# Sixteen weight units split ahead in mixer blocks one and two of a hybrid decoder layer

## The chip, the cores and the metric

The kernel runs on one core of one Trainium2 chip. The metric is the device time of one execution in microseconds (us). Five engines matter: TensorE (PE, with its weight loads as PEld), VectorE (DVE), ScalarE (ACT), GpSimd (POOL) and SyncE (SP), whose queue issues nearly all DMAs. Each engine and each queue takes its instructions in the order in which the program lists them.

## The reference

One layer of a hybrid decoder on a prompt of 2048 tokens and a sample of 8 x 4 tokens, with 1024 features:

```python
xr, gate, q, k, v = jnp.split(rmsnorm(x, g_mix) @ w_in, SPLITS, axis=-1)
y_lru = rg_lru(causal_dwconv(xr, ...), ...) * gelu(gate)       # 512 wide
y_att = sliding-window attention with sinks over q, k, v       # 512 wide
x = x + concat([y_lru, y_att]) @ w_out                         # 1024 x 1024
qc = rmsnorm(x, g_cross) @ w_mem_q                             # 1024 x 512
x = x + softmax(qc mem_k^T / sqrt(128)) mem_v @ w_mem_o        # 512 x 1024
x = x + ConvFFN(rmsnorm(x, g_ffn)); y = rmsnorm(x, ...)
```

`w_in` gives 1792 columns; the memory attention has 4 heads over 256 memory tokens. Outputs are the two y, new caches and states.

## The kernel before, in words

**Arithmetic.** Every product is made of three matmuls in fp32r: high by high, low by high, high by low (`mm3`, L137). So each operand is split: the high part is a rounding copy (ScalarE, L79), the low part the difference (L83, on GpSimd for weights, on VectorE for most activations).

**Stages.** The tokens go in four blocks of 512 (the last one is 544 with the sample). Phase 0 makes the memory keys and values (to 47 us in the profiled execution). Phase 1, the mixer, runs blocks 0 to 3 one after the other (block 1 from about 186 to 300 us, block 2 from 305 to 420, block 3 to 573); each has 14 units `unit(0)` to `unit(13)` of the input projection `w_in` (k, v, four of q, then xr and gate by turns; PSUM tile `pin`), with the window attention (`sc` scores, `tp` transposes, `po`) and the RG-LRU in between. The RG-LRU of one block is finished during the next: ScalarE makes exponentials and roots, GpSimd the products `lu` (L970), VectorE the scan (L989), GpSimd `hlast` and `gate` (L990, L991), and the result goes by DMA to `ymix` in DRAM (L996). Phase 2 (573 to about 1077 us) takes a block's `ymix` back, does the output projection (eight units of `w_out`, `out(0)` to `out(7)`, PSUM tile `po2`), the norm (`x`, `xgh`, `xgl`), the memory queries (four units of `w_mem_q`, tile `pq`), the attention and four units of `w_mem_o`, each block overlapped with the next one's output projection. Phase 3 is the ConvFFN (to the end at 2744 us).

**Weights.** A unit is 128 x 1024. `weight_order` (L85) lists all uses of phases 0 to 2 in order, and `weights` (L106) keeps two units ahead. The first time a unit is used it is loaded raw (`wr`, a pool of four buffers), split into `wh` (ScalarE) and `wl` (GpSimd), and, if it is used again, both parts are stored in DRAM (`keeph`, `keepl`, L127). At later uses the two parts are loaded (L119). The split parts lie in a pool `wspl` of three buffers for each of `wh` and `wl`, used in turn: a new tile goes into a buffer when its last reader is done. All of `w_in` is made in block 0 and reloaded in blocks 1 to 3; `w_out`, `w_mem_q` and `w_mem_o` are made when phase 2's first block reaches them, and reloaded for its other three blocks.

**Order.** A scheduler with a cost model sets the order on each engine before the run, from the order of the code and priorities; it also picks which buffer of a pool a tile takes.

Of the kernel before, what the change touches and what calls it, by code (L numbers as in the profile page):

```python
# [10 lines left out]
F = mybir.dt.float32  # L11
R = mybir.dt.float32r
# [33 lines left out]
class _Kernel:  # L46
# [38 lines left out]
    def weight_order(self):  # L85
        I = self.I
        o = [I["w_mem_k"][h] for h in range(4)] + [I["w_mem_v"][u] for u in range(4)]
        for s in range(4):
            o += [I["w_in"][u] for u in range(14)]
        o += [I["w_out"][m] for m in range(8)]  # L90
        for s in range(4):
            o += [I["w_mem_q"][h] for h in range(4)]
            if s < 3:
                o += [I["w_out"][m] for m in range(4)]
            o += [I["w_mem_o"][u] for u in range(4)]
            if s < 3:
                o += [I["w_out"][m] for m in range(4, 8)]
        self.worder, self.wq = o, []
        self.wsplit = 0
        self.wkey = lambda a: (a.tensor.name, a.offset)  # L100
        self.wkept = {}
        self.wuses = {}
        for a in o:
            self.wuses[self.wkey(a)] = self.wuses.get(self.wkey(a), 0) + 1

    def weights(self, src, ahead=2):  # L106


        nc = self.nc
        i = self.wsplit - len(self.wq)  # L110
        assert self.wkey(self.worder[i]) == self.wkey(src)
        while self.wsplit <= min(i + ahead, len(self.worder) - 1):
            unit = self.worder[self.wsplit]
            key = self.wkey(unit)
            hi = self.wspl.tile([128, 1024], R, name="wh", tag="wh")
            lo = self.wspl.tile([128, 1024], R, name="wl", tag="wl")
            if key in self.wkept:
                for t, d in zip((hi, lo), self.wkept[key]):
                    nc.sync.dma_start(t.bitcast(F), d)  # L119
            else:  # L120
                raw = self.wraw.tile([128, 1024], F, name="wr", tag="wr")
                nc.sync.dma_start(raw, unit)
                self.split(raw, hi, lo, "act", "pool" if self.wsplit > 2 else "dve")
                if self.wuses[key] > 1:
                    self.wkept[key] = [self.dram.tile([128, 1024], F, name=f"keep{e}{self.wsplit}") for e in "hl"]
                    for t, d in zip((hi, lo), self.wkept[key]):
                        nc.sync.dma_start(d, t.bitcast(F))  # L127
            self.wq.append((hi, lo))
            self.wsplit += 1
        return self.wq.pop(0)  # L130

    def mm3(self, outs, w, x, first, last, more=False):
        nc = self.nc
        combos = ((0, 0), (0, 1), (1, 0))
        for n, (a, b) in enumerate(combos):
            for o, xs in zip(outs, x[b]):
                nc.tensor.matmul(o, w[a], xs, start=first and n == 0, stop=last and n == 2, skip_group_check=more)  # L137
# [244 lines left out]
    def p1_block(self, s):  # L382
        nc, tc, I, O = self.nc, self.tc, self.I, self.O
# [10 lines left out]
        def unit(u):  # L394
            wt = self.weights(I["w_in"][u])
            ps = [self.psum([128, n], "mm", "pin") for _, n in subs]
            self.proj(wt, nh, nl, ps, subs, KT)
            return ps

        if s:  # L400
            nc.vector.tensor_copy(kh[:, 0:128], kh[:, 512:640].bitcast(F))
            nc.vector.tensor_copy(kl[:, 0:128], kl[:, 512:640].bitcast(F))
        ps = unit(0)
        if 0 < s < 3:
            self.p1_sums(s + 1)
# [4 lines left out]
        if smp:  # L410
            kf = q1.tile([128, 160], F, name="kf")
            nc.vector.tensor_copy(kf, ps[1][:, 384 - subs[1][0]:W - subs[1][0]])
            nc.sync.dma_start(O["swa_k"], kf[:, 0:128])
            nc.sync.dma_start(O["s_k_new"], kf[:, 128:160])
        ps = unit(1)
        next(fin, None)
        vt = q1.tile([128, W], F, name="vt")
# [6 lines left out]
        for j in range(4):  # L424
            ps = unit(2 + j)
            if j == 3 and s == 0:
                self.p1_sums(1)
                self.rts[1] = self.p1_rstd(1)
            h = q1.tile([128, W], R, name=f"qh{j}")
            l = q1.tile([128, W], R, name=f"ql{j}")  # L430
            for (o, n), p in zip(subs, ps):
                self.last_lo = self.split(p, h[:, o:o + n], l[:, o:o + n])
            if smp:
                f = q1.tile([128, NS], F, name=f"qf{j}")
                nc.vector.tensor_copy(f, ps[1][:, subs[1][1] - NS:subs[1][1]])
                qs.append(f)
            qh.append(h)
            ql.append(l)
            next(fin, None)
# [1167 lines left out]
```

## Time and profile before

| | |
|---|---|
| Time, median of 3 runs (lowest, highest) | 2738.78 us (2737.75, 2747.58) |
| Profiled execution: time | 2745.93 us |
| Profiled execution: span | 2744.2 us (1.7 us lie beside it) |
| TensorE busy, of the span | 2611.7 us, 95% |
| VectorE, ScalarE, GpSimd busy | 55%, 40%, 35% |
| TensorE's mean granted clock | 0.977 of full |

The profiled execution is 7.15 us longer than the median and 1.65 us shorter than the longest of the three. Times in the rows below are us from the span's start. A granted clock of 1.00 is the upper of TensorE's two levels (2.4 GHz), 0.50 the lower (1.2 GHz); a figure between them is a mean over a stretch.

### The profile page before, as it was taken

The numbers are of one execution on the slowest core, as the hardware profiler recorded it, in microseconds if no ns is written. First come the engines' busy times: TensorE is split into PE (matmuls) and PEld (weight loads), VectorE is DVE, ScalarE is ACT, GpSimd is POOL, SyncE is SP. The second block draws the span as 40 slices with busy tenths as digits, with TensorE's granted clock in tenths as the row PEclk, the third lists the DMA queues.
The fourth block names the chain that finished last, engine by engine and source line by source line (L and its number), as shares of the span: only waits on it lengthen the run. The fifth ranks groups of instructions, "written<-read, shape, count | busy, mean of one in ns | idle before, by whom it ended". The sixth has DMA issues, their size and how long they took to land.

```text
span 2744.2 us, 40972 instructions
## 1 busy us (share of the span) xinstructions
PE 2611.7 (95%) x15221; PEld 2407.4 (88%) x15221; DVE 1518.5 (55%) x2633; ACT 1085.6 (40%) x2071; POOL 954.5 (35%) x928
## 2 busy tenths in 40 slices
PE   7999999998999998888999999999999989999997
PEld 5778888977998887888999998899999989999997
DVE  6476766585442525767676755454444444444445
ACT  5454745474332434443334343333232323232233
POOL 2422211031402344466333344553232424333333
PEclk8899999998999999999999999999999999999998
DMA  6674545366747788766444487764444765444442
GB/s 234 241 230 168 183 158 173 109 243 245 258 165 245 255 268 306 272 242 209 183 161 177 146 314 252 254 216 162 150 160 158 289 214 164 159 158 167 149 154 83
DMA packets 195671, 553.72 MB, mean 202 GB/s; under 512 B 28628, under 2 KB 49364, under 8 KB 192784
## 3 DMA queue, kind: packets, MB, share of 16 engines
q1 hardware_dynamic: 195472, 551.10, 57.9%
q8 instruction: 120, 1.97, 0.3%
q14 instruction: 79, 0.65, 0.1%
HBM read 409.22 MB, written 141.80 MB: 201 GB/s over the span
## 4 chain that ended last, share of the span: by engine, by line
PE 69%; DVE 11%; DMA 6%; issue 4%; ACT 4%; POOL 4%; SPq 1%; POOLq 0%; DVEq 0%; ACTq 0%
PE pg L137 23%; PE pd L137 17%; PE pin L137 10%; PE po L137 5%; PE pmo L137 3%; PE pq L137 3%; DVE gc L1398 3%; POOL pc L83 2%; PE sc L137 1%; DMA x<-x2d 1%; ACT gc L1396 1%; DMA opd<-n3s 1%; POOL x L756 1%; POOL n3s L83 1%; PE tp L853 1%
## 5 line engine op out<-in xcount | busy, mean ns | idle before, releaser
L137 PE MATMUL pg<-n,pc 128*128 128x346 f32 (+1 forms) x6048 | 1022.0, 327 | 48.2 <-DVE up L1353 16.1
L137 PEld LDWEIGHTS pg<-n,pc 128*128 128x128 f32 x6048 | 965.6, 189 | 92.6 <-DVE up L1353 28.2
L83 POOL TENSOR_TENSOR pc<-wr,pc 128x512 fp32r<-128x512 f32 x312 | 411.0, 1322 | 451.4 <-ACT pc L79 446.2
L137 PE MATMUL pd<-ah,pc 128*128 128x346 f32 (+1 forms) x2240 | 467.7, 325 | 18.7 <-DVE acc L1422 12.9
L137 PEld LDWEIGHTS pd<-ah,pc 128*128 128x128 f32 x2240 | 379.4, 191 | 24.7 <-DVE acc L1422 17.6
L79 ACT ACTIVATE pc<-wr 128x512 fp32r<-128x512 f32 x312 | 195.3, 629 | 503.3 <-PE pd L137 236.7
L1422 DVE TENSOR_TENSOR acc<-pd,acc 128x692 f32<-128x692 f32 (+1 forms) x280 | 245.0, 878 | 175.6 <-PE pd L137 172.7
L137 PE MATMUL pd<-al,pc 128*128 128x346 f32 (+1 forms) x1120 | 271.6, 324 | 0.0
L137 PEld LDWEIGHTS pd<-al,pc 128*128 128x128 f32 x1120 | 196.6, 191 | 0.0
L1398 DVE SCALAR_TENSOR_TENSOR gc<-gb,pp,gc 128x696 f32<-128x696 f32 (+2 forms) x144 | 150.1, 1043 | 82.8 <-ACT gc L1396 79.0
L137 PE MATMUL pin<-n1h,wh 128*128 128x512 f32 (+1 forms) x560 | 188.9, 363 | 5.6 <-DVE ql L83 1.8
L137 PE MATMUL pin<-n1h,wl 128*128 128x512 f32 (+1 forms) x560 | 185.8, 358 | 2.8 <-POOL wl L83 2.8
L137 PE MATMUL pin<-n1l,wh 128*128 128x512 f32 (+1 forms) x560 | 186.6, 359 | 1.5 <-DVE n1l L83 1.5
L83 POOL TENSOR_TENSOR wl<-wr,wh 128x1024 fp32r<-128x1024 f32 x35 | 84.7, 2426 | 218.7 <-ACT wh L79 190.8
L1353 DVE TENSOR_TENSOR u<-pg,u 128x346 f32<-128x346 f32 (+1 forms) x144 | 74.3, 516 | 141.0 <-PE pg L137 140.5
L83 POOL TENSOR_TENSOR pc<-ws,pc 128x512 fp32r<-128x512 f32 x72 | 94.5, 1312 | 158.7 <-ACT pc L79 140.6
L1353 DVE TENSOR_TENSOR up<-pg,u 128x346 f32<-128x346 f32 (+1 forms) x144 | 74.1, 515 | 123.5 <-PE pg L137 123.5
L79 ACT ACTIVATE pc<-ws 128x512 fp32r<-128x512 f32 x144 | 90.0, 627 | 113.1 <-PE pg L137 70.0
L137 PEld LDWEIGHTS pin<-n1h,wh 128*128 128x128 f32 x560 | 103.1, 193 | 23.5 <-DVE ql L83 2.4
L1353 DVE TENSOR_TENSOR gb<-pg,u 128x314 f32<-128x314 f32 (+2 forms) x96 | 38.9, 426 | 145.5 <-PE pg L137 145.5
L137 PEld LDWEIGHTS pin<-n1h,wl 128*128 128x128 f32 x560 | 102.6, 193 | 18.8 <-POOL wl L83 3.8
L137 PEld LDWEIGHTS pin<-n1l,wh 128*128 128x128 f32 x560 | 102.7, 194 | 17.1 <-DVE n1l L83 2.6
(317 smaller groups left out, 4196.0 us busy)
## 6 DMA issues: line engine op xcount, KB each, us to landing
pc<-kept_s SPq DMA_DIRECT2D x192, 512.0 KB, 4.3
kept_s<-pc SPq DMA_DIRECT2D x96, 512.0 KB, 3.0
wh<-keeph SPq DMA_DIRECT2D x90, 512.0 KB, 4.0
wl<-keepl SPq DMA_DIRECT2D x90, 512.0 KB, 5.0
wr<-in_w_gate_dram SPq DMA_DIRECT2D x72, 512.0 KB, 3.8
wr<-in_w_down_dram SPq DMA_DIRECT2D x72, 512.0 KB, 4.0
opd<-n3s SPq DMA_DIRECT2D x56, 346.0 KB, 3.6
n<-opd SPq DMA_DIRECT2D x14, 1384.0 KB, 11.2
```

The lines of the kernel that those rows point to most:

```text
L79: nc.scalar.activation(hi, src, AF.Copy)
L83: return e.tensor_tensor(out=lo, in0=src, in1=hi.bitcast(F), op=OP.subtract).ins
L137: nc.tensor.matmul(o, w[a], xs, start=first and n == 0, stop=last and n == 2, skip_group_check=more)
L756: sub = lambda o, x, y, op=OP.subtract: nc.gpsimd.tensor_tensor(out=o, in0=x, in1=y, op=op)
L853: nc.tensor.transpose(tp[:, j], st[:, j, c * 128:(c + 1) * 128], K.ident)
L1353: add = lambda o, p, t: nc.vector.tensor_tensor(out=o, in0=p, in1=t, op=OP.add)
L1396: nc.scalar.activation(gc, gb[:, 2:2 + NW], AF.Identity, scale=K.col(C_FW, 48 + f), bias=K.col(C_FB, f))
L1398: nc.vector.scalar_tensor_tensor(gc, gb[:, k:k + NW], K.col(C_FW, 24 * k + f), gc, op0=OP.mult, op1=OP.add)
L1422: nc.vector.tensor_tensor(out=v, in0=pd[:, :, 0:H], in1=v, op=OP.add)
```

## The change

`wmake` and `wtiles` are cut out of `weights`, and a list `wlater` of 16 units (the eight of `w_out`, four of `w_mem_q`, four of `w_mem_o`) is made. In mixer blocks 1 and 2, after each of the units 0 to 8, one unit of the list is made: raw load, split on ScalarE and GpSimd, two stores to DRAM. That is nine units in block 1 and the seven left in block 2. The tiles come from the same pool `wspl` of three buffers. In phase 2 all units are then found in DRAM, and its first block loads both parts as the later ones do. No matmul and no split is added or taken away; 32 loads of 512 KB are added.

```diff
--- before.py
+++ after.py
@@ -100,6 +100,7 @@
         self.wkey = lambda a: (a.tensor.name, a.offset)
         self.wkept = {}
         self.wuses = {}
+        self.wlater = [I["w_out"][m] for m in range(8)] + [I["w_mem_q"][h] for h in range(4)] + [I["w_mem_o"][u] for u in range(4)]
         for a in o:
             self.wuses[self.wkey(a)] = self.wuses.get(self.wkey(a), 0) + 1
 
@@ -112,22 +113,30 @@
         while self.wsplit <= min(i + ahead, len(self.worder) - 1):
             unit = self.worder[self.wsplit]
             key = self.wkey(unit)
-            hi = self.wspl.tile([128, 1024], R, name="wh", tag="wh")
-            lo = self.wspl.tile([128, 1024], R, name="wl", tag="wl")
             if key in self.wkept:
+                hi, lo = self.wtiles()
                 for t, d in zip((hi, lo), self.wkept[key]):
                     nc.sync.dma_start(t.bitcast(F), d)
             else:
-                raw = self.wraw.tile([128, 1024], F, name="wr", tag="wr")
-                nc.sync.dma_start(raw, unit)
-                self.split(raw, hi, lo, "act", "pool" if self.wsplit > 2 else "dve")
-                if self.wuses[key] > 1:
-                    self.wkept[key] = [self.dram.tile([128, 1024], F, name=f"keep{e}{self.wsplit}") for e in "hl"]
-                    for t, d in zip((hi, lo), self.wkept[key]):
-                        nc.sync.dma_start(d, t.bitcast(F))
+                hi, lo = self.wmake(unit)
             self.wq.append((hi, lo))
             self.wsplit += 1
         return self.wq.pop(0)
+
+    def wtiles(self):
+        return [self.wspl.tile([128, 1024], R, name=n, tag=n) for n in ("wh", "wl")]
+
+    def wmake(self, unit):
+        nc, key = self.nc, self.wkey(unit)
+        raw = self.wraw.tile([128, 1024], F, name="wr", tag="wr")
+        nc.sync.dma_start(raw, unit)
+        hi, lo = self.wtiles()
+        self.split(raw, hi, lo, "act", "pool" if self.wsplit > 2 else "dve")
+        if self.wuses[key] > 1:
+            self.wkept[key] = [self.dram.tile([128, 1024], F, name=f"keep{e}{len(self.wkept)}") for e in "hl"]
+            for t, d in zip((hi, lo), self.wkept[key]):
+                nc.sync.dma_start(d, t.bitcast(F))
+        return hi, lo
 
     def mm3(self, outs, w, x, first, last, more=False):
         nc = self.nc
@@ -395,6 +404,8 @@
             wt = self.weights(I["w_in"][u])
             ps = [self.psum([128, n], "mm", "pin") for _, n in subs]
             self.proj(wt, nh, nl, ps, subs, KT)
+            if s in (1, 2) and self.wlater and u < 9:
+                self.wmake(self.wlater.pop(0))
             return ps
 
         if s:
```

In the rows of the order that follow, `pin`, `po2` and `pq2` are matmul outputs, the number behind a name tells one tile from another, and `x<-a,b` reads a and b and writes x.

The first place is SyncE's queue in block 1, around the loads of `w_in` units 5, 6 and 7 (`..._713`, `..._752`, `..._791`). Before:

```order
L119 DMA wh_1960<-keeph13_713 128x1024
L119 DMA wl_1961<-keepl13_714 128x1024
L119 DMA wh_2008<-keeph14_752 128x1024
L119 DMA wl_2009<-keepl14_753 128x1024
L996 DMA ymix0_63<-gate_963 128x512
L119 DMA wh_2049<-keeph15_791 128x1024
L119 DMA wl_2050<-keepl15_792 128x1024
L996 DMA ymix0_63<-gate_1141 128x512
L996 DMA ymix0_63<-gate_1347 128x512
```

After, the same loads, now with the stores of made units (`keeph`, `keepl` as targets) between them:

```order
L138 DMA keeph16_1958<-wh_1954 128x1024
L138 DMA keepl16_1959<-wl_1955 128x1024
L119 DMA wh_1990<-keeph5_713 128x1024
L119 DMA wl_1991<-keepl5_714 128x1024
L138 DMA keeph17_2025<-wh_2021 128x1024
L138 DMA keepl17_2026<-wl_2022 128x1024
L1007 DMA ymix0_63<-gate_963 128x512
L119 DMA wh_2048<-keeph6_752 128x1024
L119 DMA wl_2049<-keepl6_753 128x1024
```

The load of unit 6 stood ahead of the store of the first gate to `ymix`, and directly behind the load of unit 5; now it stands behind the stores of two made units and behind that gate's store.

The second place is GpSimd's queue in the same part of block 1, where the RG-LRU of block 0 is finished. Before:

```order
L170 TENSOR_TENSOR ssum_1817<-ssum_1817,sq_1851 128x512
L970 TENSOR_TENSOR lu_1052<-lu_1052,xc_919 128x512
L970 TENSOR_TENSOR lu_1243<-lu_1243,xc_1042 128x512
L970 TENSOR_TENSOR lu_1455<-lu_1455,xc_1233 128x512
L970 TENSOR_TENSOR lu_1712<-lu_1712,xc_1445 128x512
L990 COPY hlast_879<-xc_919 128x1
L991 TENSOR_TENSOR gate_963<-gate_963,xc_919 128x512
```

After:

```order
L179 TENSOR_TENSOR ssum_1827<-ssum_1827,sq_1861 128x512
L83 TENSOR_TENSOR wl_1910<-wr_1907,wh_1909 128x1024
L83 TENSOR_TENSOR wl_1955<-wr_1952,wh_1954 128x1024
L981 TENSOR_TENSOR lu_1052<-lu_1052,xc_919 128x512
L981 TENSOR_TENSOR lu_1243<-lu_1243,xc_1042 128x512
L981 TENSOR_TENSOR lu_1455<-lu_1455,xc_1233 128x512
L83 TENSOR_TENSOR wl_2022<-wr_2019,wh_2021 128x1024
L981 TENSOR_TENSOR lu_1712<-lu_1712,xc_1445 128x512
L1001 COPY hlast_879<-xc_919 128x1
L1002 TENSOR_TENSOR gate_963<-gate_963,xc_919 128x512
```

Three low parts of made units (`wl<-wr,wh`) came in ahead of the first gate, one of them between the third and the fourth product `lu`.

The third place is TensorE at the start of phase 2, where the last unit of the output projection (`po2_6330` before, `po2_6430` after) meets the first memory query (`pq2_6391`, `pq2_6485`). Before:

```order
L137 MATMUL po2_6285<-yh7_6009,wl_6186 128x512
L137 MATMUL po2_6330<-yh0_5967,wh_6230 128x512
L137 MATMUL pq2_6391<-xgh_6089,wh_6275 128x512
L137 MATMUL pq2_6391<-xgl_6090,wh_6275 128x512
L137 MATMUL pq2_6391<-xgh_6089,wl_6276 128x512
L137 MATMUL pq2_6391<-xgh_6133,wh_6275 128x512
L137 MATMUL pq2_6391<-xgl_6134,wh_6275 128x512
L137 MATMUL pq2_6391<-xgh_6133,wl_6276 128x512
```

After:

```order
L146 MATMUL po2_6391<-yh7_6157,wl_6310 128x512
L146 MATMUL po2_6430<-yh0_6115,wh_6348 128x512
L146 MATMUL pq2_6485<-xgh_6225,wh_6387 128x512
L146 MATMUL pq2_6485<-xgl_6226,wh_6387 128x512
L146 MATMUL po2_6430<-yl0_6116,wh_6348 128x512
L146 MATMUL po2_6430<-yh0_6115,wl_6349 128x512
L146 MATMUL po2_6430<-yh1_6121,wh_6348 128x512
L146 MATMUL po2_6430<-yl1_6122,wh_6348 128x512
L146 MATMUL pq2_6485<-xgh_6225,wl_6388 128x512
L146 MATMUL pq2_6485<-xgh_6263,wh_6387 128x512
L146 MATMUL pq2_6485<-xgl_6264,wh_6387 128x512
```

Before, one matmul of the last output unit is followed by the whole first query; after, the unit's next matmuls come between the query's first ones.

## Rows read from the trace of the kernel before

**Rows 1.** The page's first part, the whole span: busy time, share, instructions.

```profile
PE 2611.7 (95%) x15221; PEld 2407.4 (88%) x15221; DVE 1518.5 (55%) x2633; ACT 1085.6 (40%) x2071; POOL 954.5 (35%) x928
```

**Rows 2.** Stretches (us); busy us and instructions of each engine; granted clock (1.00 full), DMA.

```profile
core 0: us, PE busy (x) PEld busy (x) DVE busy (x) ACT busy (x) POOL busy (x), PEclk, DMA share, GB/s
...
186.00:300.00 114.00, 113.50 (x561) 92.24 (x560) 80.94 (x193) 65.53 (x157) 26.52 (x27) 1.00 0.52 176
305.00:420.00 115.00, 114.49 (x569) 93.49 (x568) 81.47 (x198) 66.22 (x159) 27.04 (x30) 1.00 0.52 177
```

**Rows 3.** ScalarE in block 1, copies of projection outputs: start, length, idle before, releaser.

```profile
220.50 0.60 ACT L79 ACTIVATE qh<-pin 128x512 fp32r<-128x512 f32 x1 [0.55 <-PE pin L137]
226.03 0.60 ACT L79 ACTIVATE qh<-pin 128x512 fp32r<-128x512 f32 x1 [4.93 <-PE pin L137]
231.56 0.60 ACT L903 ACTIVATE xr<-pin 128x512 f32<-128x512 f32 x1 [4.93 <-PE pin L137]
```

**Rows 4.** DMA issues in block 1 on SyncE's queue: start, length of the issue.

```profile
213.84 0.32 SPq L119 DMA_DIRECT2D wh<-keeph  x1
...
224.80 0.32 SPq L996 DMA_DIRECT2D ymix<-gate  x1
225.21 0.39 SPq L119 DMA_DIRECT2D wh<-keeph  x1
```

**Rows 5.** GpSimd in block 1: start, length; idle time before in brackets.

```profile
214.93 1.30 POOL L970 TENSOR_TENSOR lu<-lu,xc 128x512 f32<-128x512 f32 x1 [9.86 <-DVE xc L968]
216.85 5.56 POOL L970 TENSOR_TENSOR lu<-lu,xc 128x512 f32<-128x512 f32 x3 [0.63 <-DVE xc L968]
...
222.96 1.81 POOL L991 TENSOR_TENSOR gate<-gate,xc 128x512 f32<-128x512 f32 x1
```

**Rows 6.** DMA issues of the whole span: count, KB of each, median us to landing.

```profile
wh<-keeph SPq DMA_DIRECT2D x90, 512.0 KB, 4.0
wl<-keepl SPq DMA_DIRECT2D x90, 512.0 KB, 5.0
...
keeph<-wh SPq DMA_DIRECT2D x30, 512.0 KB, 3.5
keepl<-wl SPq DMA_DIRECT2D x30, 512.0 KB, 2.9
```

**Rows 7.** Weight splits, ScalarE's high part, 560 to 730: ns min/median/max, first and last start.

```profile
L79 ACT ACTIVATE wh<-wr x14: 1042/1056/1066, 569.6 to 710.2; 128x1024 fp32r<-128x1024 f32 x14
```

**Rows 8.** Weight splits, GpSimd's low part, 560 to 730, in the same columns.

```profile
L83 POOL TENSOR_TENSOR wl<-wr,wh x14: 2357/2399/3422, 570.8 to 711.3; 128x1024 fp32r<-128x1024 f32 x14
```

**Rows 9.** Stretches at the start of phase 2.

```profile
570.00:657.00 87.00, 76.86 (x297) 59.64 (x297) 55.97 (x87) 49.51 (x75) 32.98 (x22) 0.88 0.70 254
574.00:600.00 26.00, 26.00 (x118) 21.06 (x117) 16.19 (x25) 25.41 (x36) 7.49 (x3) 1.00 0.92 323
629.00:636.00 7.00, 6.08 (x15) 4.77 (x15) 2.66 (x3) 0.98 (x2) 0.37 (x1) 0.51 1.02 414
646.00:657.00 11.00, 9.93 (x28) 8.19 (x29) 5.51 (x8) 4.33 (x7) 3.38 (x2) 0.53 0.53 191
```

**Rows 10.** What TensorE waited for, 559 to 730: us, times, longest.

```profile
PE pq L137 <- POOL wl L83: 2.8, 2, 1.8
PE pq L137 <- issue: 2.3, 1, 2.3
PE pq L137 <- ACT xgh L1142: 1.7, 1, 1.7
...
PE pq L137 <- DVE xgl L1143: 0.9, 1, 0.9
PE pq L137 <- ACT wh L79: 0.9, 1, 0.9
...
PE po L137 <- POOL wl L83: 0.5, 1, 0.5
```

**Rows 11.** A stretch of block 0, in which every weight unit is made.

```profile
78.00:95.00 17.00, 17.00 (x76) 13.63 (x75) 2.08 (x3) 4.78 (x7) 7.16 (x3) 1.00 0.70 270
```

## The prediction

> **What bounds the kernel now.** I read the page first: TensorE is busy for 95% of the span and no other engine for more than 55% [rows 1], so time is lost or won only where TensorE waits or where its clock falls. Next the table by stretches. In mixer blocks 1 and 2, where the new work goes, TensorE is busy 113.50 of 114 us and 114.49 of 115, at a granted clock of 1.00 [rows 2]; there is nothing to win there, and any delay adds to the time one for one. ScalarE is busy for 65.53 us and GpSimd for 26.52 us of block 1's 114 [rows 2], so both have room. At the start of phase 2, where work is taken away, TensorE is busy 76.86 of 87 us at a mean clock of 0.88 [rows 9]: 10.1 us idle and, since a stretch at half clock loses half of itself, about 0.12 x 87 = 10.4 us of clock. Two of the slow stretches are in the rows: 7 us at 0.51 and 11 us at 0.53 [rows 9]. So 20.5 us is all that phase 2's start can give. The list of waits then says how much of the idle time the weight splits end: 2.8 + 0.5 us for the low parts and 0.9 for a high part, 4.2 us; 1.7 and 0.9 us end with the activations `xgh` and `xgl`, 2.3 us with nothing shown [rows 10].
>
> **What is taken from phase 2's start.** Sixteen splits go from ScalarE and GpSimd, 1.056 us and 2.40 us each [rows 7, 8], together 17 us of ScalarE and 38 us of GpSimd. Fourteen of them lie between 560 and 730 us. ScalarE was busy 25.41 of 26 us from 574 to 600 [rows 9], while it also finished block 3's RG-LRU and split the inputs of the output projection, so its other work there comes some microseconds earlier. In place of one raw load and two stores a unit has two loads, which take 4.0 and 5.0 us to land [rows 6], two units ahead; that is inside the 5.53 us of a unit (the copies of successive outputs start at 220.50, 226.03 and 231.56 [rows 3]) even when the ring gives only one unit's lead, within 0.5 us. The order also interleaves the last output unit with the first query, so that the query no longer waits in one piece in front of work that is ready. Direct gain: the 4.2 us of waits on splits. Beyond it, part of the remaining 5.9 us of idle time and of the 10.4 us of clock, since the slow stretches follow the idle ones. The lower bound is 0 (VectorE's scan and the norm could hold the queries just as long), the upper 20.5; I take the middle, 10, as the splits end 4.2 of the 9.1 us that the list names, a little under half.
>
> **What is added in blocks 1 and 2.** The same 16 splits, with their loads and stores. TensorE, ScalarE and GpSimd get no more work than before in total. GpSimd's nine low parts in block 1 are 21.6 us, and its 26.52 us become 48 of 114; by share this is hidden. What is not hidden is order, at three places.
>
> First the ring. The made units take buffers of the same three as the loads of `w_in`, and hold one for most of units 3 to 8: high part 1.06 us, low part 2.40, issue 0.3 to 0.4, store 2.9 to land, so a buffer is free again 5.7 us after the low part starts [rows 4, 6 to 8]. The loads of `w_in` are left with two, so a load can go out when the unit two before has ended, and must land within one unit: 0.32 + 0.4 of issue and 5.0 of landing are 5.7 us against 5.53 [rows 3, 4, 6]. Alone that is a wait of 0.2 us a unit, 6 units a block: 1 us.
>
> Second, SyncE's queue. Behind each store of a made unit, which waits for ScalarE or GpSimd, stands the next load of `w_in`, and TensorE waits for that. The worst place is unit 6. Before, its load was issued at 213.84 [rows 4], twelve microseconds before TensorE wanted it, at the end of unit 5 about 226.0 [rows 3]. After, it stands behind `keeph17`, `keepl17` and the first gate's store, as the order shows. Third, GpSimd's queue: that gate's product ended at 222.96 + 1.81 = 224.8, its store went out at 224.80 [rows 4, 5], and now three low parts of 2.40 us stand ahead of it. The first two can use the 9.86 us in which GpSimd was idle before the first `lu` [rows 5], if ScalarE makes their high parts in time; the third lies between the products and is paid in full. So the gate ends at 224.8 + 2.4 = 227.2 if both are hidden, at 232.0 if neither. I take one of the two as hidden: 229.6. The load's issue follows 0.4 us later and the high part lands 4.0 us on, at 234.0; TensorE could have gone on at 226.0. The scores that the scheduler moved between unit 6's first matmuls fill the further 1.5 us until the low part is there. That makes a wait of 8.0 us in block 1 (5.6 to 10.4), and waits at units 3 to 5 are inside it, since the gate does not wait for those units. Block 2 has the same sequence with seven units: another 8.0. Together 16 us, against nothing if the queues have enough slack and 20.8 + 2 if not. Nothing in block 3 or phase 3 moves.
>
> By the row, the low part takes 2.357 to 3.422 us, the median 2.399 [rows 8], and I count the median. The Trainium skill's page "GPSIMD Engine Reference" (section 1, Specifications) has it that GpSimd's SBUF interface is shared with VectorE and contends with VectorE instructions that have two SBUF inputs. VectorE is busy 80.94 of 114 us in block 1 [rows 2]; were every low part there as slow as the slowest in the row, the two that I count ahead of the gate would cost 1.0 us more each, 2 us a block and 4 in the sum.
>
> **Sum.** 16 added, 10 taken: the profiled execution's 2745.93 would be 2752. That execution is 7.15 us above the median, within the spread of the three runs, so I forecast the median plus 6, 2738.78 + 6 = 2745 us.
>
> **Rivals.**
>
> Hidden: the queues have slack and blocks 1 and 2 take no longer. For it speaks block 0: from 78 to 95 us, where every unit is loaded raw, split and stored, TensorE is busy 17.00 of 17 us at full clock [rows 11]. Against it, there the RG-LRU of a block before is not being finished, and the split unit is itself the one needed, so the ring holds nothing else. With no wait, and 10 to 20 us gained, middle 14: 2725 us.
>
> Slower, by the clock: a wait of TensorE in a block at full clock is followed by a slow stretch. The two stretches in phase 2's start cost 0.49 x 7 = 3.4 and 0.47 x 11 = 5.2 us [rows 9], and both follow idle time. With two such stretches in each block, at 4.3 us, and the waits at 10.4: 20.8 + 17.2 - 10 = 28, 2767 us. It decides where one wait of several microseconds stands in a block; whether TensorE still has scores to run is what speaks against it. The page "TensorE: Matmul & The Clock Gate" of the Trainium skill (section "HAM oscillation — how this bites in real kernels") describes this for matmuls that wait for data in every tile, where each tile then begins at the slow clock; the rows agree in so far as the slow stretches here lie behind waits.
>
> Slower, without the gain: the queries wait for the scan and the norm as long as before, and only the 16 us and a part of the 4.2 count: 16 - 2 = +14, 2753 us.
>
> **How the numbers follow.** The forecast has 0.43 (its own range 2736 to 2755), hidden 0.25, the clock 0.20, no gain 0.12. About 0.5%, 13.7 us, is what a measurement of this kernel can tell from no change: 2725 to 2752. Faster by more than that is half of hidden and a little of the forecast, 0.16; slower is nearly all of the clock, half of no gain and a fifth of the forecast, 0.33; the rest, 0.51, lies between. The range of 2722 to 2768 takes in most of hidden and most of the clock.
>
> **What would show it.** In blocks 1 and 2 of the changed profile: TensorE's waits for `wh` and `wl` by DMA at unit 6, some 8 us each, against none now; the load of unit 6 issued only behind the gate's store, near 230 us; the blocks' windows 8 us longer. At phase 2's start: no wait on a split by ScalarE or GpSimd, idle time near 5 us in place of 10.1, clock above 0.88. The forecast is wrong if TensorE stays at 99% through units 3 to 9 (hidden), if the granted clock drops below 1.00 there (the clock), or if the queries still start as late after the last output unit.

## The result, and the profile after

The changed kernel takes 2776.17 us (median of 4 runs, 2773.21 to 2778.73) against 2740.61 before (four runs). The medians lie 35.6 us apart; the ratio on record is 1.0111 [1.0089, 1.0133], which is 30 us slower. The kernel before has medians of 2745.5 to 2747.8 us in the later runs of the experiments, so the four runs here are lower than most. The forecast was 2745 and its range ended at 2768, so the time lies above it; slower by more than 0.5% had a chance of 0.33 in it.

The page's first part, of the changed kernel's profiled execution (2773.21 us, span 2771.4):

```profile
PE 2617.5 (94%) x15221; PEld 2410.2 (87%) x15221; DVE 1516.1 (55%) x2633; ACT 1086.7 (39%) x2071; POOL 952.8 (34%) x928
```

TensorE's busy time grew by 5.8 us in all [rows 1], the span by 27. Where, the stretches tell. First two stretches of the kernel before, each from the first matmul of a block's unit 0 to that of the next block's (busy us of PE, PEld, DVE, ACT, POOL; granted clock; DMA):

```profile
185.80:304.70 118.90, 118.41 (x589) 96.44 (x588) 85.36 (x205) 67.77 (x161) 26.52 (x27) 1.00 0.52 177
304.70:424.20 119.50, 118.99 (x593) 97.27 (x592) 85.95 (x208) 68.15 (x162) 27.04 (x30) 1.00 0.52 177
```

The same two of the changed kernel, and the start of its phase 2, placed as the 87 us of [rows 9] are:

```profile
181.90:322.90 141.00, 128.19 (x589) 101.36 (x588) 94.21 (x206) 76.45 (x170) 47.94 (x36) 0.93 0.72 250
322.90:463.70 140.80, 127.43 (x593) 101.22 (x592) 93.88 (x208) 75.28 (x169) 44.15 (x37) 0.94 0.67 230
610.90:697.90 87.00, 82.63 (x379) 67.30 (x378) 56.09 (x114) 51.45 (x90) 5.88 (x12) 0.96 0.72 247
```

Blocks 1 and 2 take 141.0 and 140.8 us in place of 118.9 and 119.5: 43 us more. Of these 25 us are idle time of TensorE (12.8 and 13.4 against 0.5 and 0.5), and the clock of 0.93 and 0.94 is 9.9 + 8.4 = 18 us more. The busy time says the same: as many matmuls (589 and 593) keep TensorE busy for 9.8 and 8.4 us longer. At phase 2's start 4.4 us are idle in place of 10.1 and the clock is 0.96 in place of 0.88: 13 us back. The two windows don't hold the same work (297 and 379 matmuls), but the whole of phase 2, from its first output-projection matmul to its last of `w_mem_o`, says the same: 503.8 us before, 490.2 after, 13.6 back. What TensorE waited for in block 1:

```profile
PE pin L146 <- DMA wh<-keeph: 8.1, 1, 8.1
PE tp L864 <- DVE S L854: 3.2, 3, 1.3
PE pin L146 <- ACT vt L430: 1.4, 1, 1.4
```

In block 2:

```profile
PE pin L146 <- DMA wh<-keeph: 5.7, 1, 5.7
PE tp L864 <- DVE S L854: 3.0, 3, 1.0
PE pa L146 <- ACT gate L939: 1.5, 1, 1.5
PE pin L146 <- ACT vt L430: 1.2, 1, 1.2
PE pvt L813 <- DVE ptl L83: 1.1, 1, 1.1
```

At the start of phase 2, where no split is waited for any more [rows 10]:

```profile
PE pq L146 <- DMA wh<-keeph: 2.1, 1, 2.1
PE pq L146 <- ACT xgh L1153: 1.7, 1, 1.7
```

The wait of 8.1 us is unit 6 of block 1. Its first matmul:

```profile
238.36 0.77 PE L146 MATMUL pin<-n1h,wh 128*128 128x512 f32 x1 [8.13 <-DMA wh<-keeph]
```

The stretch at half clock (0.50) that starts within the wait:

```profile
232.00:245.70 13.70, 7.34 (x20) 5.63 (x21) 6.02 (x19) 2.28 (x9) 8.60 (x9) 0.50 0.85 266
```

SyncE's queue there, start and length:

```profile
220.12 0.32 SPq L138 DMA_DIRECT2D keeph<-wh  x1
228.92 0.32 SPq L138 DMA_DIRECT2D keepl<-wl  x1
233.35 0.32 SPq L1007 DMA_DIRECT2D ymix<-gate  x1
233.76 0.38 SPq L119 DMA_DIRECT2D wh<-keeph  x1
```

GpSimd at the same time:

```profile
219.93 3.38 POOL L981 TENSOR_TENSOR lu<-lu,xc 128x512 f32<-128x512 f32 x2 [3.88 <-DVE xc L979]
223.94 1.68 POOL L981 TENSOR_TENSOR lu<-lu,xc 128x512 f32<-128x512 f32 x1 [0.63 <-DVE xc L979]
225.58 3.32 POOL L83 TENSOR_TENSOR wl<-wr,wh 128x1024 fp32r<-128x1024 f32 x1
228.86 2.18 POOL L981 TENSOR_TENSOR lu<-lu,xc 128x512 f32<-128x512 f32 x1
...
232.07 1.26 POOL L1002 TENSOR_TENSOR gate<-gate,xc 128x512 f32<-128x512 f32 x1
```

ScalarE's copy of unit 5's output, which comes at its end or, with ScalarE busy, a little later:

```profile
229.89 0.58 ACT L79 ACTIVATE qh<-pin 128x512 fp32r<-128x512 f32 x1
```

The queue reads as forecast: `keepl` waits for the low part that stands between the products, the gate's store (233.35) for the gate behind it, and the load of unit 6 goes out at 233.76. Unit 5 had ended at 229.6; after three score matmuls TensorE stood idle from 230.2 for the 8.1 us.

### The profile page after: what moved, and what is told of

It is laid out like the page before. It is cut to its first block, busy times and chain, and to the rows that moved or that the text cites. A ratio compares the mean times of both kernels' runs of the same rounds, so it can differ in the third digit from the quotient of the medians.

```text
span 2771.4 us, 41012 instructions
## 1 busy us (share of the span) xinstructions
PE 2617.5 (94%) x15221; PEld 2410.2 (87%) x15221; DVE 1516.1 (55%) x2633; ACT 1086.7 (39%) x2071; POOL 952.8 (34%) x928
## 4 chain that ended last, share of the span: by engine, by line
PE 54%; DVE 7%; DMA 5%; issue 4%; POOL 4%; ACT 3%; SPq 1%; POOLq 0%; DVEq 0%; ACTq 0%
PE pg L146 24%; PE pd L146 17%; PE po L146 4%; PE pq L146 3%; PE pmo L146 3%; DVE gc L1409 3%; POOL pc L83 2%; ACT gc L1407 1%; DMA opd<-n3s 1%; POOL n3s L83 1%; DMA x<-x2d 1%; DMA wr<-in_w_up_dram 1%; POOL x L767 1%; PE msc L146 1%; DVE up L1364 1%
```

## The experiments

The stages of every kernel's profile are worked out from its matmuls: a block from the first matmul of unit 0 to that of the next block, block 3 to the first output-projection matmul, and phase 2's start from there to the first memory transpose. Ratios are to the kernel before on the same chip, with the 95% interval. Stage times are of one profile each and move by some us without an edit: block 0 takes 135.1 to 139.1 us in the kernels that make nothing ahead there, and phase 2's start took 88.2 us in `twice` with the same waits on splits as before. The last column also overstates the gain: of its 16.9 us (changed), the stretch behind it, to the next block's first transpose, takes 3 back (109.5 us before, 112.5 after).

| kernel | ratio | block 0 | block 1 | block 2 | phase 2's start |
|---|---|---|---|---|---|
| before | 1 | 138.8 | 118.9 | 119.5 | 91.8 |
| changed | 1.0111 [1.0089, 1.0133] | 135.6 | 141.0 | 140.8 | 75.0 |
| no_make | 0.9965 [0.9952, 0.9977] | 135.9 | 119.0 | 119.5 | 77.0 |
| twice | 1.0134 [1.0115, 1.0154] | 135.1 | 138.7 | 139.8 | 88.2 |
| in_raw | 1.0036 [1.0023, 1.0048] | 143.6 | 128.7 | 122.0 | 75.2 |
| st_pool | 1.0176 [1.0158, 1.0193] | 136.6 | 150.9 | 149.5 | 76.1 |
| held | 1.0003 [0.9992, 1.0015] | 136.6 | 125.1 | 126.8 | 76.7 |
| low_dve | 1.0038 [1.0024, 1.0051] | 135.6 | 133.4 | 130.5 | 76.5 |
| no_store | 1.0085 [1.0067, 1.0102] | 136.1 | 134.8 | 136.5 | 76.0 |
| no_store_dve | 1.0056 [1.0040, 1.0071] | 135.8 | 134.2 | 134.1 | 75.2 |
| in_raw_dve | 1.0051 [1.0037, 1.0066] | 138.3 | 130.6 | 133.1 | 76.0 |
| late | 1.0035 [1.0021, 1.0048] | 136.7 | 128.5 | 132.1 | 75.2 |
| in_raw_late | 1.0049 [1.0036, 1.0061] | 144.3 | 134.0 | 125.1 | 76.6 |
| spread | 1.0031 [1.0018, 1.0044] | 135.8 | 119.7 | 127.8 | 76.9 |
| spread_dve | 1.0024 [1.0011, 1.0037] | 138.0 | 118.7 | 124.7 | 78.2 |
| gain_eight | 0.9971 [0.9958, 0.9983] | 139.1 | 119.7 | 120.7 | 75.7 |
| sparse | 0.9972 [0.9961, 0.9983] | 136.2 | 119.2 | 124.5 | 75.0 |

**Do the two sides add up?** Two kernels, one with the gain alone and one with the cost alone. `no_make` maps the sixteen units to kept parts of `w_in`:

```diff
-            if s in (1, 2) and self.wlater and u < 9:
-                self.wmake(self.wlater.pop(0))
+            if s == 2 and u == 13:
+                for i, v in enumerate(self.wlater):
+                    self.wkept[self.wkey(v)] = self.wkept[self.wkey(I["w_in"][i % 14])]
```

> Leaves out the splits of the 16 units: phase 2's first block loads parts of w_in units in their place. It shows what phase 2's start gains by itself. If the two sides add up: blocks 1 and 2 as before (119 us each), and 12 us less from block 3 on, 2728. If the gain in the changed kernel is only a shift (phase 2's start profits because the RG-LRU of block 3 ran at another time): 2735 to 2741.

`twice` forgets the made units, so that phase 2 makes its own:

```diff
+                v = self.wlater.pop(0)
+                self.wmake(v)
+                self.wkept["m", self.wkey(v)] = self.wkept.pop(self.wkey(v))
```

> Blocks 1 and 2 make and store the 16 units as in the changed kernel, but phase 2 makes them again as before. It shows the cost of the making by itself. If the two sides add up: blocks of 141 us each and the start of phase 2 as before, 2740 + 43 = 2783. If part of the cost is another clock state of phase 2 or block 3: outside 2776 to 2790.

Both came out as if they add, within their intervals: `no_make` is 0.35% (some 10 us) faster with blocks of 119, `twice` 1.34% (37 us) slower with 40 us in the two blocks and 88 us at phase 2's start. So the making costs about 40 us and buys about 10, or 13 by the stages; a state of the clock carried from one stage into another isn't needed to explain the result.

**Which resource?** Four kernels, of which three each take one away and one (`held`) keeps one alone. Each edit also gives the scheduler's order another shape, so a difference is that of the edit and of the new order together. `in_raw`, made units outside the ring:

```diff
+        if made:
+            hi, lo = self.wraw.tile([128, 1024], R, name="wrh", tag="wr"), raw.bitcast(R)
+        else:
+            hi, lo = self.wtiles()
```

> The made units use two buffers of the raw pool each (the high part in one, the low part written over the raw unit), so the three buffers of wspl belong to w_in again; the stores stay on SyncE's queue. Theory (the loads of w_in are late because the made units hold one buffer of the ring): the waits for wh by DMA at unit 6 (8.1 and 5.7 us after) go, blocks 1 and 2 come back from 141 us each to 119 to 122, the clock there to 0.99 or more, and with the 12 us gained behind them the time is 2727 to 2735 against 2740. Rival (SyncE's queue alone: loads stand behind stores that wait for GpSimd): waits of several us stay at some units, blocks of 128 to 135 us, 2750 to 2765. Rival (ScalarE's and GpSimd's work itself delays scores and gates): blocks stay near 141, 2770.

Blocks 1 and 2 of `in_raw` fell to 128.7 and 122.0: 31 of the 43 us are gone. But the kernel is still slower than before (1.0036), where the theory had it faster, and block 0 is 143.6 us. The free raw buffers let the scheduler pull making forward into block 0:

```profile
47.00:185.80 138.80, 128.14 (x555) 102.02 (x556) 81.53 (x185) 62.88 (x140) 41.86 (x28) 0.86 0.67 234
```

and `in_raw`, with its block 2:

```profile
46.50:190.00 143.50, 127.65 (x555) 101.18 (x554) 85.11 (x184) 67.59 (x145) 58.49 (x35) 0.88 0.74 265
...
318.80:440.80 122.00, 119.41 (x594) 97.04 (x593) 89.57 (x209) 69.14 (x163) 32.60 (x32) 1.00 0.65 218
```

GpSimd's 41.86 us became 58.49. Its low parts of made units in block 0 and in block 1:

```profile
L83 POOL TENSOR_TENSOR wr<-wr,wrh x6: 2375/2408/2460, 140.6 to 185.2; 128x1024 fp32r<-128x1024 f32 x6
...
L83 POOL TENSOR_TENSOR wr<-wr,wrh x9: 2387/2406/3607, 233.7 to 316.2; 128x1024 fp32r<-128x1024 f32 x9
```

Six of the sixteen begin in block 0, nine in block 1 and one in block 2, and none in units 0 to 4 of either block; in the changed kernel nine are in block 1 and seven in block 2, from unit 1 on. So `in_raw` moved the making as well as taking it out of the ring. The waits for `wh` at unit 6 are gone, but this run doesn't show that the ring caused them: block 2 came back to 122 us with one unit made in it, and no low part stands ahead of the first gate any more. The splits in block 0 cost where they now stand.

`held`, the ring of two alone: one pair of buffers is filled at unit 1 and released after unit 8, on top of `no_make`:

```diff
+            if s in (1, 2) and u == 1:
+                self.held = self.wtiles()
+                for t, d in zip(self.held, self.wkept[self.wkey(I["w_in"][0])]):
+                    nc.sync.dma_start(t.bitcast(F), d)
+            if s in (1, 2) and u == 8:
+                for k, t in enumerate(self.held):
+                    nc.vector.tensor_copy(t[:, 0:1], ps[0][:, 0:1])
+                    d = self.dram.tile([128, 1024], F, name=f"held{s}{k}")
+                    nc.sync.dma_start(d, t.bitcast(F))
```

> Leaves out the splits as no_make does, and in blocks 1 and 2 loads one pair of buffers of wspl at unit 1 that stays taken until unit 8 (two one-column copies on VectorE, two loads and two stores a block): the ring of two for w_in alone, with no split, no store of a made unit between the loads, and nothing added to GpSimd. If the ring of two is most of the 22 us a block: the load of unit 6 still goes out only behind the first gate's store, waits of 3 to 6 us at units 6 to 8, blocks of 127 to 138 us. If the stores in SyncE's queue and the late gate on GpSimd are most of it: 119 to 123 us a block.

Measured: 125.1 and 126.8 us, 13.5 more in the two, between the two cases. Its waits in both blocks, and SyncE's queue at unit 6:

```profile
PE pin L146 <- DMA wh<-keeph: 6.6, 2, 3.6
```

```profile
212.45 0.32 SPq L119 DMA_DIRECT2D wh<-keeph  x1
...
223.42 0.32 SPq L1017 DMA_DIRECT2D ymix<-gate  x1
223.85 0.37 SPq L119 DMA_DIRECT2D wh<-keeph  x1
```

With no split and no store, the load of unit 6 already goes out behind the gate's store, at 223.85 in place of right behind the load of unit 5 at 212.45. So a ring of two is enough to put the load behind the gate's store, and by itself costs a third of the 43 us.

`low_dve`, low parts of made units on VectorE:

```diff
-        self.split(raw, hi, lo, "act", "pool" if self.wsplit > 2 else "dve")
+        self.split(raw, hi, lo, "act", "pool" if self.wsplit > 2 and not made else "dve")
```

> The changed kernel with the low parts of the 16 made units on VectorE instead of GpSimd. If GpSimd's queue (the gate behind three low parts, one of them 3.3 us long between the products) decides, the wait at unit 6 falls from 8.1 us to 2 to 4 and blocks to 128 to 136 us. If ring and SyncE's queue decide whatever makes the low part: the wait stays at 6 to 9 us and blocks at 138 to 145.

```profile
PE pin L146 <- DMA wh<-keeph: 10.2, 2, 5.3
PE tp L864 <- DVE S L854: 2.7, 4, 1.0
```

The waits at unit 6 are 5.3 and 4.9 us, less than after, more than expected; the blocks are 18 us shorter than in the changed kernel. GpSimd's queue is a part.

`st_pool`, the stores issued by GpSimd:

```diff
-                nc.sync.dma_start(d, t.bitcast(F))
+                (nc.gpsimd if made else nc.sync).dma_start(d, t.bitcast(F))
```

> The changed kernel with the stores of the made units issued by GpSimd instead of SyncE; the ring is shared as in the changed kernel. Ring theory: loads of w_in still have two buffers, blocks 1 and 2 stay above 130 us, 2755 to 2775. Rival (SyncE's queue): no load stands behind a store any more, blocks of 119 to 125 us, 2728 to 2742. If GpSimd's queue (the gate behind three low parts) decides, the wait at unit 6 stays at 6 to 9 us and the others go: blocks of 128 to 133 us.

This was worse than all expected, 150.9 and 149.5 us. GpSimd in block 1 (busy, mean ns, idle before it):

```profile
L83 POOL TENSOR_TENSOR wl<-wr,wh 128x1024 fp32r<-128x1024 f32 x9 | 22.2, 2471 | 41.0 <-ACT wh L79 22.7 <-DMA keepl<-wl 18.1
...
L138 POOL DMA_DIRECT2D keeph<-wh x9 | 5.3, 584 | 8.9 <-ACT wh L79 8.9
```

Each issue takes 0.58 us of GpSimd, and the issues wait for ScalarE (8.9 us) in GpSimd's queue. It doesn't clear SyncE's queue either: there the raw loads of made units now wait 27.7 us in block 1 for GpSimd's low parts (11.0 the longest), and loads of `w_in` stand behind them. The Trainium skill's page "DMA: Bandwidth & Descriptors" (section "Issuing engines are not separate DMA queues") says that starting DMAs from several engines at once saves only the time that it takes to issue them. This run saved nothing by it: the two blocks took 19 us more than in the changed kernel.

**Are they separate prices?** `no_store` leaves the stores out:

```diff
+                raw = self.wraw.tile([128, 1024], F, name="wr", tag="wr")
+                nc.sync.dma_start(raw, v)
+                hi, lo = self.wtiles()
+                self.split(raw, hi, lo, "act", "pool")
```

> Leaves out the 32 stores of the made units (phase 2 loads parts of w_in units in their place); raw loads, ScalarE's high parts, GpSimd's low parts and the shared buffers of wspl stay. A buffer is then free when the low part is done, not 3 us later, and the order puts the load of unit 6 ahead of the first gate's store again; GpSimd still has three low parts ahead of that gate. If SyncE's queue and the time that a buffer is held decide: no wait of several us at unit 6, blocks of 119 to 125 us. If GpSimd's and ScalarE's own work decides: blocks of 130 to 141.

It gave back 10.6 us; the blocks lie in the second case's range. With 13.5 for the ring and 17.9 for the low parts that is 42 of 43, which looked like a sum. `no_store_dve` takes two of them away at once (the last word above is then `"dve"`):

> Leaves out the stores of the made units (as no_store) and makes their low parts on VectorE (as low_dve); the shared ring and ScalarE's high parts stay. In the profiles the ring alone cost 13.5 us of blocks 1 and 2 (held), taking the low parts off GpSimd gave back 17.9 of the 43 (low_dve), leaving the stores out 10.6 (no_store). If these three add up, blocks 1 and 2 together are 253 us here, 14 to 15 more than before. If they share one wait (the load of unit 6), removing two of them leaves nearly nothing: 239 to 245. If something else remains (ScalarE's high parts): 258 or more.

The blocks are 268.3 us together: 30 more than before, and 4.4 more than with the low parts alone moved. They are not separate prices. Where the wait went, SyncE's queue shows:

```profile
224.45 0.32 SPq L120 DMA_DIRECT2D wh<-keeph  x1
...
229.13 0.32 SPq L1016 DMA_DIRECT2D ymix<-gate  x1
...
230.21 0.32 SPq L120 DMA_DIRECT2D wh<-keeph  x1
234.29 3.64 SPq L1016 DMA_DIRECT2D ymix<-gate  x2
238.02 0.38 SPq L120 DMA_DIRECT2D wl<-keepl  x1
```

```profile
PE pin L147 <- DMA wl<-keepl: 12.0, 3, 6.4
```

The load of unit 6 is nearly in time (224.45; a wait of 0.5 us). But the low part of unit 7's is issued at 238.02, behind the stores of two gates, and TensorE waits for it 5.1 us in block 1 and 6.4 in block 2. One wait was exchanged for another, one unit on. What this kernel still adds in blocks 1 and 2 is the ring, the raw loads, ScalarE's high parts and the low parts on VectorE; no kernel here takes the high parts away, so their share stays open.

`in_raw_dve` took away ring and GpSimd together:

> Made units in buffers of the raw pool and their low parts on VectorE: neither ring nor GpSimd is touched, ScalarE's high parts, the raw loads and the stores on SyncE's queue stay. If ring and GpSimd's queue together are the cost: blocks 1 and 2 at 119 to 121 us. If in_raw's longer block 0 (143.6 us against 136 to 139) comes from raw loads and splits that the free raw buffers let in early: block 0 stays at 142 or more, and the whole at 2738 to 2745 against 2745. If GpSimd was the cause there, block 0 is back at 137 and the time at 2730 to 2736.

```profile
PE pr L198 <- POOL ssum L182: 7.3, 2, 4.5
PE pin L149 <- DMA wh<-keeph: 5.8, 2, 5.5
```

Block 0 is back though five units are still split in it, which fits GpSimd's low parts as what lengthened it in `in_raw`. But the blocks are 25 us longer, not 0 to 3: a wait for the sums (7.3 us in two) and one for a high part (5.5). That ring and GpSimd's queue together are the cost falls with this run.

**Another place for the making.** `late` puts it at units 5 to 13 of blocks 1 and 2 (`u > 4` in place of `u < 9`):

> The changed kernel with the making moved from units 0 to 8 to units 5 to 13 of blocks 1 and 2; ring, queues and the number of made units are the same. Units 9 to 13 start 10 to 11 us apart, not 5.5, and the products and gates are mostly done. If a ring of two hurts only where a load must land within one unit of 5.53 us: no wait at unit 6, blocks of 119 to 124 us, and 13 us gained behind them: 2728 to 2740. If a made unit costs the same wherever it stands: blocks near 141, 2770.

22 us in the two blocks, half of the change's cost, though units there are far apart:

```profile
PE pin L146 <- DMA wh<-keeph: 4.1, 2, 3.0
PE pr L195 <- POOL ssum L179: 3.1, 1, 3.1
PE pin L146 <- DMA wl<-keepl: 1.6, 1, 1.6
```

GpSimd in block 2 of `late`, at the sums for the next block's norm:

```profile
322.91 5.01 POOL L179 TENSOR_TENSOR ssum<-ssum,sq 128x544 f32<-128x544 f32 x3 [17.98 <-ACT sq L178]
```

The waits for `w_in` parts now stand at unit 8 of either block, behind the last gates' stores and those of the first made units, and TensorE waits for the sums in block 2. No low part stands in front of these: GpSimd was idle for 18.0 us before them and waited for ScalarE's squares. What made the squares late is not shown. `in_raw_late`, both edits:

> Both: made units in buffers of the raw pool, and at units 5 to 13. in_raw kept 9.8 us in block 1 (a wait of 2.2 us of the sums, one at half clock) and 2.5 in block 2. If these come from made units beside the sums, products and gates: blocks of 119 to 121 us, 2726 to 2735. If from the added DMAs anywhere in the block: 122 to 128 us, 2740.

It has 20.7 us in blocks 1 and 2 and 144.3 in block 0; the expectation failed, and six splits pulled into block 0 by the free raw buffers are again there (nine in block 1, one in block 2).

`spread` keeps clear of the first eight units of every block:

```diff
-            if s in (1, 2) and self.wlater and u < 9:
+            if s and self.wlater and (u > 8 or (s == 3 and u == 8)):
```

> The changed kernel with five units made at units 9 to 13 of blocks 1 and 2 and six at units 8 to 13 of block 3; ring, queues and engines are as in the changed kernel. Units there start 10 to 11 us apart and GpSimd is idle for nearly all of 250 to 300 us before. If a ring of two and GpSimd's queue cost only between units 3 and 8: blocks 1 and 2 at 119 to 122 us, the gain of 13 us behind them kept: 2730 to 2737 against 2745. If each made unit costs about 2.7 us wherever it stands (43 over 16): 2775.

```profile
182.60:302.20 119.60, 118.61 (x589) 96.24 (x588) 87.53 (x204) 72.69 (x166) 39.28 (x32) 1.00 0.67 232
302.20:430.00 127.80, 122.39 (x594) 98.08 (x593) 87.95 (x207) 76.01 (x169) 40.70 (x35) 0.99 0.68 234
430.00:586.00 156.00, 146.18 (x1015) 134.43 (x1014) 101.76 (x264) 82.47 (x208) 29.68 (x30) 0.94 0.57 195
```

Block 1 with its five units costs 0.8 us. Block 2 costs 8.3 and block 3 6.8 by the same measure (156.2 us against 149.4). The gain at phase 2's start was kept and the kernel was still slower than before. `spread_dve`:

> As spread, with the low parts of made units on VectorE. If GpSimd's copies of the last columns (carry, xr) behind a low part hold up the convolution in units 9 to 13: 2 to 4 us a block less than spread. If VectorE's score work is held up instead: as much more.

Block 2 is 3 us shorter than in `spread`, block 3 is 5.6 us longer (161.8); in total no difference that the intervals would show.

**Fewer units.** `gain_eight` asks which units carry the gain (as `no_make`, with eight units in the list):

> As no_make, but only the last four units of w_out and the four of w_mem_q are left unsplit; the first four of w_out and the four of w_mem_o are made in phase 2 as before. If the gain of 15 to 17 us between the first output-projection matmul and the first memory transposes comes from the units that TensorE waits for there: 76 to 79 us for that stretch. If ScalarE's and GpSimd's relief from 570 to 600 us by the first units is what counts: 83 us or more.

The stretch is 75.7 us: the eight units that stand where TensorE waited give all of it. So `sparse` makes only those ahead, one after every second unit:

```diff
-        self.wlater = [I["w_out"][m] for m in range(8)] + ...
+        self.wlater = [I["w_out"][m] for m in range(4, 8)] + [I["w_mem_q"][h] for h in range(4)]
-            if s in (1, 2) and self.wlater and u < 9:
+            if s and self.wlater and u in (8, 10, 12):
```

> Only those eight units are made ahead, after units 8, 10 and 12 of blocks 1, 2 and two of block 3, from the shared ring, stores on SyncE's queue. spread cost 16 us for 16 units (9 in blocks 1 and 2, 7 in block 3). If a unit out of two leaves room: cost 0 to 4 us, gain 8 to 12 us, 2734 to 2742 against 2746. If each made unit costs 1 us there: cost 8, gain 8 to 12, same.

```profile
183.20:302.40 119.20, 118.72 (x590) 96.31 (x589) 89.63 (x204) 70.80 (x165) 33.93 (x30) 1.00 0.65 219
302.40:426.90 124.50, 121.80 (x594) 98.24 (x593) 90.63 (x208) 73.91 (x167) 34.91 (x33) 0.99 0.61 206
579.80:654.90 75.10, 71.17 (x318) 56.99 (x317) 46.79 (x88) 46.85 (x78) 10.80 (x13) 0.98 0.81 272
```

Block 1 is as before, block 2 costs 5.0 us, block 3 is 3.6 longer (153.0), phase 2's start gives 16.8. Block 3's part isn't shown to be the making's: `gain_eight`, which makes nothing ahead, has 153.5 us there with the same two longest waits (3.5 and 1.8 us; 3.3 and 1.8 in `sparse`). The same holds for part of the 6.8 in `spread`. The time is 2738.66 us against 2745.64 on the same chip, ratio 0.9972 [0.9961, 0.9983]: faster than before by 0.3%, and faster than the changed kernel, whose interval begins at 1.0089. It is the ratio of `gain_eight` too (0.9971), so what making the eight units costs here doesn't show in the time. `sparse` differs from the changed kernel in the number of units and in their places; eight units at units 0 to 8 were not run, so which of the two counts for more is open.

## Why the prediction was wrong, point by point

**What bounds the kernel** held: blocks 1 and 2 had no room, and every delay there came back one for one and more.

**The gain at phase 2's start** was right: forecast 10 of at most 20.5 us, measured 13 (13.6 over the whole of phase 2); idle 4.4 us (forecast near 5), clock 0.96, no wait on a split. Every kernel with this gain also has the interleaved order of the last output unit and the first query, so what that order alone gives was not told apart.

**The wait at unit 6** was right in place and cause, behind the gate's store and the low part between the products. Its size, 8.0 us forecast and 8.1 and 5.7 measured, was luck in block 1. Counted from the block's start, the high part was there at 56.5 us (238.36) where I had 48.2, and TensorE was ready for it at 48.3 where I had 40.2: both ends came 8 us late, and only their difference was right.

**The step that failed is the next one: "Together 16 us".** That wait was taken for the whole price of the two blocks, which was 43. Two terms were missing. By the profiles the blocks cost 27 us more than forecast, phase 2 gave 4 more and block 0 was 3 us shorter; with smaller differences elsewhere that makes the 21 us from 2752, the sum for the profiled execution, to 2773. Another 7 us of the miss are the step from that sum to a median: I took off the 7.15 us by which the profiled execution lay above a median of three, and the later medians, 2745.5 to 2747.8, don't bear that out.

The clock, 18 us. I had it as a rival, with two slow stretches a block at 4.3 us, and left it out of the forecast although the forecast itself held a wait of 8 us a block, and rows 9 showed slow stretches behind waits. The profile after has a clock of 0.93 and 0.94 over the two blocks. The rival's 2767 (17.2 us of clock) was nearest to the result; it had the clock nearly right and the waits too small by 4 us. The granted clock was 0.50 from 232.0 to 245.7 us, from within the wait of 8.1 us to 7 us behind it. The Trainium skill's page "TensorE: Matmul & The Clock Gate" (section "HAM oscillation — how this bites in real kernels") has matmuls that wait for data start again at the slow clock. The trace agrees, and where the blocks wait little, the clock stays (1.00 in block 2 of `in_raw` and block 1 of `sparse`). No run changes the clock alone, so that the waits bring it down is what all runs fit, not a thing shown by itself.

The other waits, 11 to 12 us. "Waits at units 3 to 5 are inside it, since the gate does not wait for those units" was false. Block 1 begins at 185.8 before and 181.9 after. The gate's product ended 39.0 us into the block before [rows 5] and 51.4 after: 12.4 later, where I had 4.8; the first product `lu` is already 8.9 us later (219.93 against 214.93 [rows 5]), and the copy of unit 5's output 7.8 (229.89 against 226.03 [rows 3]). The transposes that the scheduler moved ahead wait 3.2 and 3.0 us for VectorE, and unit 3 waits 1.4 and 1.2 us for ScalarE's copy of `vt`, which stands behind a made unit's high part (and, as before, behind four other instructions). So early delays had moved the gate too, and were paid in addition. A smaller part is that the loads of `w_in` land later in blocks 1 and 2, where 12 raw loads and 32 stores were added: median 4.6 and 5.8 us for high and low part, against 3.8 and 4.9 before. It isn't the reason for the wait at unit 6: in `held` they land in 3.7 and 5.0 us, and unit 6 still waits 3.6 and 3.0 us. That ScalarE's roots carried the delay from TensorE to the products, because they stand in its queue behind copies of TensorE's outputs, is read from the order and not shown by a run.

**The ring, SyncE's queue and GpSimd's queue as three places** was right as a list and wrong as a sum to be made term by term: the ring, priced at 1 us a block, has 13.5 us by itself in two, and the edits do not add up. What stays open is which one order would be free of waits with sixteen units; no kernel here had that.

**VectorE beside GpSimd.** The low parts of blocks 1 and 2 in the changed kernel (ns min/median/max):

```profile
L83 POOL TENSOR_TENSOR wl<-wr,wh x16: 2336/2408/3318, 189.6 to 399.5; 128x1024 fp32r<-128x1024 f32 x16
```

The one in front of the gate was a slow one, 3.32 us at 225.58. The Trainium skill's page "GPSIMD Engine Reference" (section 1, Specifications) has GpSimd's SBUF interface shared with VectorE and contended by VectorE instructions with two SBUF inputs. The trace agrees: the three slowest low parts (2.84, 3.25 and 3.32 us) ran beside VectorE's scan of `la` and `lu` (L1000), and the fastest, 2.34 us at 235.57, with VectorE idle. It is a part of 1 us in 43.

**The other rivals.** "Hidden" fell; what spoke for it, block 0's full pace while making every unit [rows 11], says nothing where the RG-LRU's chain and a gate's store stand in the same queues. "Without the gain" fell too.

## What to carry to other kernels

Idle engines were not free room here: the work put on them took buffers and places in queues that go in order, and its price was seen in what stands behind the new instruction in each queue, not in the engine's share. Where a forecast holds a wait of several us in a stage at full clock, a slow stretch behind it belongs in the same sum; here it was 18 us on 25 us of idle time. If work must be made ahead, make only the part that was waited for, and put it where the ring and the queues have a whole unit to spare: eight units so placed gained 0.3%, sixteen in a row lost 1.1%. And where an edit frees buffers, look where the scheduler has put the work before reading the stages: in `in_raw` six units had moved into block 0.

## What the runs showed of the hardware

A DMA issued by GpSimd occupied it for 0.58 us (`keeph`, nine in block 1), where an issue of such a store on SyncE's queue took 0.32. GpSimd's subtraction of one unit, 2.34 us at its fastest, took up to 3.32 beside VectorE's scan. Both are small against the time that they held up what was queued behind them.
